# A two-block transformer on one core: scores per head on 64 rows, normalisation on VectorE, and another machine model in the scheduling pass

## The chip, the cores and the metric

The kernel runs on one core of a Trainium2 chip. The metric is the device time of the whole program in microseconds (us), measured from several runs; one further run is profiled, and the rows below come from it. The engines are TensorE (PE, with its weight loads PEld), VectorE (DVE), ScalarE (ACT), GpSimd (POOL) and SyncE (SP, which issues the DMAs). Each engine works through its own queue in order and waits on semaphores for the others.

## What is computed

256 tokens of width 1024 go through two blocks and a final norm. What matters here are the three attentions; all heads have 64 channels.

```
# block 0, NSA: 16 query heads, 4 key heads; branches: compressed, selected, window
q  = rms_norm(to_heads(q, 16), q_gain) * 64 ** -0.5
ks = rms_norm(to_heads(ks, 4), k_gain[1]); kw = rms_norm(to_heads(kw, 4), k_gain[2])
s  = einsum('bgrqd,bgqnld->bgrqnl', q, k_g) - slopes * dist     # causal, per head
p  = masked_softmax(s)
o  = gate0 * o_compressed + gate1 * o_selected + gate2 * o_window
# block 0, further: out-projection, experts (MoE), a per-layer embedding (PLE)
# block 1, moba: 16 query heads, 4 shared key heads, one softmax per head; out-projection, MoE, PLE, ffn1
# mixer: half of the width by pooling, half by 8 heads with decayed scores; ffn2; final norm
```

With 256 tokens the selected blocks and the window hold all earlier tokens, so that both branches are causal softmaxes over 256 keys with an ALiBi term.

## The kernel before

**Products.** Everything is float32. A dense layer splits each operand into a high and a low part and adds three products (`mm3`, L305 to L307: hi with hi, hi with lo, lo with hi). Weights come by DMA into tiles of the tag `raw` (9 slots), in units of at most 128x2048; `halves` splits each unit into `hi` (ScalarE, L292) and `lo` (VectorE, L293). The tag `a` names four banks of PSUM, `b` the other four; dense layers with tokens on the partitions write `a`.

**Keys.** `kb` is a tile of the tag `raw` too. In before it holds, for each of four pairs of heads, two copies of the keys of 256 tokens: one with zeros in the partitions 64 to 127 and one with zeros in 0 to 63. The zeros are written by two memsets on GpSimd (L545) when the program asks for the tile; `put_k` then writes the keys after their transposes (L348), head by head, L557 on ScalarE and L559 on VectorE.

**The way to the keys.** In NSA: the compression of keys and values (L642, then a gelu over L645 to L649, then small products L652, L666, L670 and L683), and `k_T`: squares on ScalarE (L494), sums on VectorE (L495), an inverse square root by three Newton steps on VectorE (L315 to L324), the scaling (L536), eight transposes on TensorE (L348), `put_k`. In moba the same `k_T` follows the dense layer `w_kv`. In program order `k_T` stands before the next dense layer (NSA: the window part of `w_a_in`; moba: `w_b_q`).

**One softmax** (`softmax_T`, 28 times: 16 in NSA, 8 in moba, 4 in the mixer) is two heads by 256 queries: scores for the first 128 queries against 128 keys (L566) and for the other 128 against 256 keys (L568), both heads by one product each, since the zeros of `kb` keep the heads apart; the mask and ALiBi term with the row maximum on VectorE (L575); the exponential on ScalarE (L580); the normalisation of four blocks, the first by ScalarE (L593) and three by VectorE (L595); six transposes (L599 to L601); a copy on ScalarE (L602); the products with the values (L609, L611), where the two heads write partitions 0 to 63 and 64 to 127.

**Order.** The program is written with a tile framework. A list scheduler decides the order of the instructions of every engine before the kernel runs: it plays the program on a machine model, gives tiles their slots as the program asks for them, and picks among ready instructions by priority (program order, moved forward by `ahead_by`). On the chip the queues run in that order.

**Ahead of ffn1 and ffn2** stands `modulated_T`: 16 transposes of the residual stream (L420), and two of its statistics (L421), one for each 128 tokens.

Of the kernel before, what the change touches and what calls it, by code (L numbers as in the profile page):

```python
# [8 lines left out]
F32 = mybir.dt.float32  # L9
# [3 lines left out]
AF = mybir.ActivationFunctionType  # L13
OP = mybir.AluOpType
AX = mybir.AxisListType

P = 128
T = 256
# [5 lines left out]
K = dict(  # L24
    raw=9,
    e=7,
    w4=5,
    load_at=[1, 1],
    over_at=1,
    defer=0,  # L30
    kinds='rwwrererrrrwrr',
    mid='e',
# [8 lines left out]
    fine=1,  # L41
    fmod=0,
    ada_eng='ppppvvppvvvvppvvpv',
    sw='svvv',
    hp={'rstd': 30, 'silu': 200, 'qn': 100, 'finish': 300, 'split': 60, 'gain': 200},
    keep=[0, 0],
    xlo='g',
# [150 lines left out]
class Block:  # L198
# [340 lines left out]
        for i in range(2):  # L539
            self.put_k(4 * br + 2 * i, self.transposed(kdf, i), gain)  # L540

    def keys(self):
        kb = self.raw.tile([P, 4, 2, T], F32, tag="raw", name="kb")
        for hf in range(2):
            self.nc.gpsimd.memset(kb[64 * hf:64 * hf + 64, :, 1 - hf], 0.0)  # L545
        return kb

    def put_k(self, idx, ps, gain):

        nc = self.nc  # L550
        for hf, eng in ((0, "s"), (1, "v")):
            sl = slice(64 * hf, 64 * hf + 64)
            dst = self.KB[idx // 4][sl, idx % 4:idx % 4 + 2, hf, :]
            if gain is None:
                self.copy(dst, ps[sl])
            elif eng == "s":
                nc.scalar.activation(dst, ps[sl], AF.Identity, scale=gain[sl])  # L557
            else:
                nc.vector.tensor_scalar(dst, ps[sl], gain[sl], None, op0=OP.mult)  # L559

    def softmax_T(self, j, kb, QT, slopes, dist, mult, gate):

        nc = self.nc
        with self.ahead_by("soft"):
            s0 = self.psa([P, 2, P])
            nc.tensor.matmul(s0, QT[:, j, 0:P], kb[:, :, 0:P], start=True, stop=True)  # L566
            s1 = self.psa([P, 2, T])
            nc.tensor.matmul(s1, QT[:, j, P:T], kb, start=True, stop=True)  # L568
            m = self.stat([P, 4], "m")
            p = self.pp_p.tile([P, 6 * P], F32, tag="p", name="p")  # L570
            p0, p1 = p[:, 0:2 * P].rearrange("p (h k) -> p h k", h=2), p[:, 2 * P:].rearrange("p (h k) -> p h k", h=2)
            blocks = [(p0[:, 0], s0[:, 0], P, 2 * P), (p0[:, 1], s0[:, 1], P, 2 * P),
                      (p1[:, 0], s1[:, 0], 0, 2 * P), (p1[:, 1], s1[:, 1], 0, 2 * P)]
            for i, (p, s, a, b) in enumerate(blocks):
                nc.vector.tensor_tensor_reduce(out=p, in0=s, in1=dist[:, a:b], scale=-float(slopes[2 * j + i % 2]),  # L575
                                               scalar=3e38, op0=OP.add, op1=OP.min, accum_out=m[:, i:i + 1])
            den = self.stat([P, 4], "den")
            for i, (p, s, a, b) in enumerate(blocks):
                if mult is None:
                    nc.scalar.activation(p, p, AF.Exp, bias=m[:, i:i + 1], scale=-1.0, accum_out=den[:, i:i + 1])  # L580
                else:
                    nc.scalar.activation(p, p, AF.Exp, bias=m[:, i:i + 1], scale=-1.0)
                    nc.vector.tensor_tensor_reduce(out=p, in0=p, in1=mult[:, a:b], scale=1.0, scalar=0.0,
                                                   op0=OP.mult, op1=OP.add, accum_out=den[:, i:i + 1])
            w = self.stat([P, 4], "w")
            nc.vector.tensor_scalar(den, den, 1e-30, None, op0=OP.max)
            nc.vector.reciprocal(w, den)
            if gate is not None:
                nc.vector.tensor_tensor(w.rearrange("p (t h) -> p t h", t=2), w.rearrange("p (t h) -> p t h", t=2),
                                        gate, op=OP.mult)  # L590
            for i, (p, s, a, b) in enumerate(blocks):
                if K["sw"][i] == "s":
                    nc.scalar.activation(p, p, AF.Copy, scale=w[:, i:i + 1])  # L593
                else:
                    self.engine(K["sw"][i]).tensor_scalar(p, p, w[:, i:i + 1], None, op0=OP.mult)  # L595
            pT = self.pp_p.tile([P, 2, 3 * P], F32, tag="pT", name="pT")
            for hh in range(2):
                ps = self.psb([P, 3 * P])
                nc.tensor.transpose(ps[:, 0:P], p0[:, hh], self.ident)  # L599
                nc.tensor.transpose(ps[:, P:2 * P], p1[:, hh, 0:P], self.ident)  # L600
                nc.tensor.transpose(ps[:, 2 * P:], p1[:, hh, P:T], self.ident)  # L601
                nc.scalar.activation(pT[:, hh], ps, AF.Copy)  # L602
        return pT

# [115 lines left out]
    def nsa(self):  # L720
        nc = self.nc
# [8 lines left out]
        x, = self.gained_T([self.c("first_gain")], K["head"]["nsa"])  # L730
# [30 lines left out]
        compress = self.compress(two)  # L761
        off = self.dense(x, "w_a_in", [512], put_sel, off, after=lambda: next(compress))
        next(compress)
        self.KB = [self.keys() for _ in range(2)]
        self.k_T(0, ks, self.s("a_k_norm1"))
        kw = self.w4([P, 2, 256])
        off = self.dense(x, "w_a_in", [304, 256], put_win, off)
# [2 lines left out]
        QT = self.e([P, 8, T])  # L770
# [36 lines left out]
    def moba(self):  # L807
        nc = self.nc
        xk, xq = self.gained_T([self.s("kv_norm"), self.s("ln_mix1")], K["head"]["moba"])
        r = self.rstd()  # L810
        k = self.w4([P, 2, 256])
        V = self.e([P, 2, 256])

        def put_kv(ci, t, ps):
            self.copy(k[:, t], ps[:, 0:256], r[:, t:t + 1])
            self.copy(V[:, t], ps[:, 256:512], r[:, t:t + 1])

        self.dense(xk, "w_kv", [512], put_kv, head=K["head"]["moba"])
        self.KB = [self.keys()]
        self.k_T(0, k, self.s("k_norm_shared"))  # L820
        qg = self.q_gain(self.s("b_q_norm"), self.c("qsc"))
        QT = self.e([P, 8, T])
        off = 0
        q = [self.w4([P, 2, 512]) for _ in range(2)]
        for c in range(2):
            off = self.dense(xq, "w_b_q", [512], lambda ci, t, ps: self.copy(q[c][:, t], ps, r[:, t:t + 1]), off)
            if c == 0:
                self.q_norm(q[c])
        self.q_T(QT, 0, q[0], qg)
        aT = (self.e([P, KT, T], F32R), self.e([P, KT, T], F32R))  # L830
        for j in range(8):
# [12 lines left out]
        self.moe(1, aT, "w_b_out")  # L844
# [694 lines left out]
    def mixer(self):  # L1539
        nc = self.nc  # L1540
        x = self.modulated_T(self.mods[:, 4], self.mods[:, 3], ("mixer", 0), K["head"]["mixer"])
        A = self.A["mixc"]
        o, n = self.m_at["band"]
# [9 lines left out]
        u, v = both[:, 0], both[:, 1]  # L1553
        QT = self.e([P, 4, T])
# [6 lines left out]
                nc.scalar.activation(QT[:, 2 * b + j], ps[:, j], AF.Identity, scale=self.c("qsc2", 2 * b + j, 2 * b + j + 1))  # L1561

        self.dense_T(x, "w_m_in", 4, put_q, per)
        self.KB = [self.keys()]
        self.dense_T(x, "w_m_in", 4, lambda b, ps: self.put_k(2 * b, ps, None), 2 * per)
        self.dense(x, "w_m_in", [512], lambda ci, t, ps: self.copy(v[:, t], ps), off=3 * per)
        aT = (self.e([P, KT, T], F32R), self.e([P, KT, T], F32R))
        for g in range(4):
            sl = slice(g * P, (g + 1) * P)
            ps = self.psb([P, T])  # L1570
# [4 lines left out]
            ps = self.psb([P, T])  # L1575
# [3 lines left out]
                                           op0=OP.mult, op1=OP.subtract)  # L1579
# [88 lines left out]
```

## Time and profile before

| what | value |
|---|---|
| median of 3 runs | 1143.19 us (1141.0 to 1143.75) |
| the profiled execution's own time | 1141.74 us |
| its span, first to last instruction | 1139.9 us |
| mean granted clock of TensorE | 0.973 |
| TensorE busy | 1061.5 us (93%) |
| VectorE, ScalarE, GpSimd busy | 729.1, 514.6, 74.8 us |

The stages in that execution: `w_a_in` and the compression to 84 us, NSA's attention to 157, its out-projection to 199, MoE to 320, PLE and moba's dense layers to 384, moba's attention to 414, out-projection to 450, MoE to 582, PLE to 607, ffn1 to 826, the mixer to 926, ffn2 to 1126, the final norm. Busy time of PE is modelled at the ends of products, so that a busy PE can still have room; waits are read from the time lines.

### The profile page before, as it was taken

How to read it: one execution, taken by the hardware profiler on the slowest of the kernel's cores; microseconds unless marked ns; L12 is line 12 of the kernel's file. 1: busy time of each engine (PE TensorE's matmuls, PEld its weight loads, DVE VectorE, ACT ScalarE, POOL GpSimd, SP SyncE). 2: the span in 40 equal slices, each digit the busy share in tenths (PEclk: the TensorE clock that was granted, in tenths of full speed). 3: DMA queues.
4: the chain of work that ended last, by engine and by line, in shares of the span. 5: the costliest groups of instructions: out<-in, count | busy, mean ns of one | idle time of the engine just before them, and what ended most of it. 6: DMA issues, size and time to landing. Idle time of an engine off the chain costs nothing.

```text
span 1139.9 us, 18296 instructions
## 1 busy us (share of the span) xinstructions
PE 1061.5 (93%) x7037; PEld 830.7 (73%) x7037; DVE 729.1 (64%) x1717; ACT 514.6 (45%) x992; POOL 74.8 (7%) x61
## 2 busy tenths in 40 slices
PE   7997999998899899998987999999989979999995
PEld 5884557564467667665555999999879759999994
DVE  6787866542379957343377587878674776554555
ACT  5446774221267774321253443443544634444443
POOL 3000002100010002000003000000210030000001
PEclk9998999997999999999998999999989989999998
DMA  9755464899964635898886468786674344454401
GB/s 372 287 194 223 186 231 154 300 383 371 350 245 166 245 126 187 327 372 318 333 322 265 148 239 332 302 308 252 234 300 168 129 184 145 169 189 164 141 26 38
DMA packets 46507, 268.55 MB, mean 236 GB/s; under 512 B 5328, under 2 KB 7120, under 8 KB 20432
## 3 DMA queue, kind: packets, MB, share of 16 engines
q1 hardware_dynamic: 46416, 267.34, 62.4%
q8 instruction: 57, 0.93, 0.3%
q14 instruction: 34, 0.28, 0.1%
HBM read 266.27 MB, written 1.05 MB: 235 GB/s over the span
## 4 chain that ended last, share of the span: by engine, by line
PE 47%; DVE 5%; ACT 1%; issue 0%; ACTq 0%; DVEq 0%
PE b L306 8%; PE b L305 8%; PE b L307 8%; PE a L305 5%; PE a L307 5%; PE a L306 5%; PE a L1055 1%; DVE nq L320 1%; PE b L1461 1%; DVE h L1484 1%; PE a L1095 1%; PE a L1108 1%; DVE rstd L324 1%; DVE w L1483 1%; PE b L1034 0%
## 5 line engine op out<-in xcount | busy, mean ns | idle before, releaser
L293 DVE TENSOR_TENSOR lo<-raw,hi 128x1024 fp32r<-128x1024 f32 (+2 forms) x220 | 255.9, 1167 | 166.5 <-ACT hi L292 165.7
L292 ACT ACTIVATE hi<-raw 128x1024 fp32r<-128x1024 f32 (+2 forms) x234 | 234.3, 1008 | 266.2 <-PE b L306 142.5
L305 PE MATMUL b<-e,hi 128*128 128x256 f32 x768 | 219.8, 286 | 2.9 <-ACT e L427 2.9
L306 PE MATMUL b<-e,hi 128*128 128x256 f32 x768 | 219.5, 286 | 0.1
L307 PE MATMUL b<-e,lo 128*128 128x256 f32 x768 | 219.1, 285 | 0.0
L305 PE MATMUL a<-hi,e 128*128 128x512 f32 (+2 forms) x512 | 201.5, 394 | 2.4 <-ACT e L365 1.8
L307 PE MATMUL a<-hi,e 128*128 128x512 f32 (+2 forms) x512 | 198.4, 390 | 0.5 <-DVE e L366 0.5
L306 PE MATMUL a<-lo,e 128*128 128x512 f32 (+2 forms) x512 | 198.9, 388 | 0.0
L305 PEld LDWEIGHTS b<-e,hi 128*128 128x128 f32 x768 | 149.4, 195 | 3.9 <-ACT e L427 3.6
L306 PEld LDWEIGHTS b<-e,hi 128*128 128x128 f32 x768 | 149.4, 194 | 1.0 <-DVE e L428 0.7
L307 PEld LDWEIGHTS b<-e,lo 128*128 128x128 f32 x768 | 149.3, 194 | 0.0
L305 PEld LDWEIGHTS a<-hi,e 128*128 128x128 f32 x512 | 97.4, 190 | 23.2 <-ACT e L365 2.9
L307 PEld LDWEIGHTS a<-hi,e 128*128 128x128 f32 x512 | 96.7, 190 | 21.3 <-DVE e L366 2.1
L306 PEld LDWEIGHTS a<-lo,e 128*128 128x128 f32 x512 | 97.6, 191 | 19.0 <-DVE lo L293 0.9
L1055 PE MATMUL a<-raw,e 128*32 128x256 f32 x832 | 78.6, 399 | 5.5 <-PEq L1314 5.4
L1055 PEld LDWEIGHTS a<-raw,e 128*32 128x32 f32 x832 | 32.2, 113 | 23.9 <-issue 9.0
L1439 DVE SCALAR_TENSOR_TENSOR w<-raw,c,w 128x512 f32<-128x512 f32 x63 | 45.7, 747 | 0.6
L485 DVE TENSOR_TENSOR h<-h,a 128x512 f32<-128x512 f32 x48 | 31.9, 684 | 21.0 <-PE a L1108 14.4
L580 ACT ACTIVATE p<-p,m 128x128 f32<-128x128 f32 (+1 forms) x96 | 42.6, 447 | 5.5 <-DVE m L575 4.4
L293 POOL TENSOR_TENSOR lo<-raw,hi 128x1024 fp32r<-128x1024 f32 (+1 forms) x14 | 31.4, 2263 | 206.1 <-ACT hi L292 206.0
L1098 ACT ACTIVATE w<-a,sv 128x512 fp32r<-128x512 f32 x32 | 21.6, 687 | 50.0 <-PE a L1095 49.0
L1084 ACT ACTIVATE hb<-a,rr 128x128 f32<-128x128 f32 x16 | 6.0, 373 | 83.6 <-DVE rr L1024 77.2
(321 smaller groups left out, 1455.9 us busy)
## 6 DMA issues: line engine op xcount, KB each, us to landing
raw<-in_ffn SPq DMA_DIRECT2D x62, 1024.0 KB, 4.8
raw<-in_moe_gu SPq DMA_DIRECT2D x52, 1024.0 KB, 7.3
raw<-in_w_ada SPq DMA_DIRECT2D x36, 1024.0 KB, 6.7
wd<-in_moe_dn SPq DMA_DIRECT2D x64, 512.0 KB, 6.1
raw<-in_w_gate SPq DMA_DIRECT2D x8, 1024.0 KB, 10.8
raw<-in_w_m_in SPq DMA_DIRECT2D x8, 1024.0 KB, 7.3
raw<-in_w_a_in SPq DMA_DIRECT2D x7, 1024.0 KB, 11.0
e<-in_moe_gu SPq DMA_DIRECT2D x6, 1024.0 KB, 6.7
```

The costliest lines, as they stand in the source:

```text
L292: nc.scalar.activation(hi[:, sl], raw[:, at], AF.Copy)
L293: eng.tensor_tensor(lo[:, sl], raw[:, at], hi[:, sl], op=OP.subtract)
L305: mm(out, l[0], r[0], start=start, stop=False, **kw)
L306: mm(out, l[0], r[1], start=False, stop=False, **kw)
L307: mm(out, l[1], r[0], start=False, stop=stop, **kw)
L320: nc.vector.scalar_tensor_tensor(q, y, h, y, op0=OP.mult, op1=OP.mult)
L324: nc.vector.scalar_tensor_tensor(y, q, 1.5, y, op0=OP.add, op1=OP.mult)
L485: self.nc.vector.tensor_tensor(self.h[:, t, sl], self.h[:, t, sl], ps, op=OP.add)
L580: nc.scalar.activation(p, p, AF.Exp, bias=m[:, i:i + 1], scale=-1.0, accum_out=den[:, i:i + 1])
L1055: nc.tensor.matmul(pgs[pp][32 * x:32 * x + 32], xg[:, k, o:o + 32], wg[kk][:, x], start=(k == 0), stop=(k == KT - 1))
L1098: nc.scalar.activation(yh[:, sl], py, AF.Identity, scale=cw)
L1439: eng.scalar_tensor_tensor(rows, w, by, rows, op0=OP.mult, op1=OP.add)
```

## The change

Four things change at once. (1) Scores are computed per head: a product per head and per half of the queries, on the 64 partitions of that head, heads alternating, each head into its own bank of PSUM. (2) So `kb` needs no zeros: the two memsets for each tile are gone, NSA's two tiles become one, and `put_k` is one copy of 128x512 by the engine whose turn it is. (3) All four blocks of a softmax are normalised by VectorE. (4) The scheduling pass uses its time-line machine model. Below line 545 the new file's numbers are smaller by 3 to 7.

```diff
-    sw='svvv',
+    sw='vvvv',
...
-    def keys(self):
-        kb = self.raw.tile([P, 4, 2, T], F32, tag="raw", name="kb")
-        for hf in range(2):
-            self.nc.gpsimd.memset(kb[64 * hf:64 * hf + 64, :, 1 - hf], 0.0)
-        return kb
+    def keys(self, n):
+
+        kb = self.raw.tile([P, n, 4, T], F32, tag="raw", name="kb")
+        self.KB = [kb[:, i] for i in range(n)]
 
     def put_k(self, idx, ps, gain):
 
-        nc = self.nc
-        for hf, eng in ((0, "s"), (1, "v")):
-            sl = slice(64 * hf, 64 * hf + 64)
-            dst = self.KB[idx // 4][sl, idx % 4:idx % 4 + 2, hf, :]
-            if gain is None:
-                self.copy(dst, ps[sl])
-            elif eng == "s":
-                nc.scalar.activation(dst, ps[sl], AF.Identity, scale=gain[sl])
-            else:
-                nc.vector.tensor_scalar(dst, ps[sl], gain[sl], None, op0=OP.mult)
+        dst = self.KB[idx // 4][:, idx % 4:idx % 4 + 2]
+        if gain is None:
+            self.copy(dst, ps)
+        else:
+            self.copy(dst, ps, gain)
...
-            s0 = self.psa([P, 2, P])
-            nc.tensor.matmul(s0, QT[:, j, 0:P], kb[:, :, 0:P], start=True, stop=True)
-            s1 = self.psa([P, 2, T])
-            nc.tensor.matmul(s1, QT[:, j, P:T], kb, start=True, stop=True)
+            s = [self.psa([P, 3 * P]) for _ in range(2)]
+            for t in range(2):
+                for hh in range(2):
+                    sl = slice(64 * hh, 64 * hh + 64)
+                    nc.tensor.matmul(s[hh][:, t * P:t * P + (t + 1) * P], QT[sl, j, t * P:(t + 1) * P],
+                                     kb[sl, 0:(t + 1) * P], start=True, stop=True)
...
-            for i, (p, s, a, b) in enumerate(blocks):
-                if K["sw"][i] == "s":
-                    nc.scalar.activation(p, p, AF.Copy, scale=w[:, i:i + 1])
-                else:
-                    self.engine(K["sw"][i]).tensor_scalar(p, p, w[:, i:i + 1], None, op0=OP.mult)
+            for i, (o, x, a) in enumerate(blocks):
+                self.engine(K["sw"][i]).tensor_scalar(o, o, w[:, i:i + 1], None, op0=OP.mult)
...
-        self.KB = [self.keys() for _ in range(2)]
+        self.keys(2)
         self.k_T(0, ks, self.s("a_k_norm1"))
...
-    with tile.TileContext(nc) as tc:
+    with tile.TileContext(nc, schedule_with_timeline_sim=True) as tc:
```

The order of the queues at three places. The first is the compression's end in NSA, on ScalarE's queue; `hi<-raw 128x608` and `128x512` are splits of the window part of `w_a_in`. Before:

```order
L292 ACTIVATE hi<-raw 128x608 x4
L645 ACTIVATE x_398<-b 128x256
L648 ACTIVATE x_398<-x_398 128x256
L292 ACTIVATE hi<-raw 128x512
L658 ACTIVATE w_407<-b 128x4x16
L292 ACTIVATE hi<-raw 128x512
L658 ACTIVATE w_407<-b 128x4x16
L675 ACTIVATE w_434,kcs<-b 128x64
L494 ACTIVATE w_463<-w_241 128x256
L494 ACTIVATE w_466<-w_241 128x256
L292 ACTIVATE hi<-raw 128x512
```

And now:

```order
L638 ACTIVATE x_398<-b 128x256
L641 ACTIVATE x_398<-x_398 128x256
L651 ACTIVATE w_407<-b 128x4x16 x2
L668 ACTIVATE w_434,kcs<-b 128x64
L494 ACTIVATE w_458<-w_241 128x256
L494 ACTIVATE w_461<-w_241 128x256
L665 ACTIVATE vc<-b 128x256
L262 ACTIVATE kb<-b,small 128x512
L292 ACTIVATE hi<-raw 128x608 x4
L292 ACTIVATE hi<-raw 128x512 x3
```

The first four splits stood ahead of the gelu (L645, now L638) and now stand behind the copy into kb. On TensorE's queue at the same place, where L642 (now L635) is the compression's first product, the new order is:

```order
L635 MATMUL b<-raw,e 64x256 x32
L645 MATMUL b<-consts,x_398 128x128 x2
L659 MATMUL b<-small,w_407 128x64
L663 MATMUL b<-small,w_408 128x64
L659 MATMUL b<-small,w_407 128x64
L663 MATMUL b<-small,w_408 128x64 x7
L676 MATMUL b<-consts,kd 128x128
L348 MATMUL b<-consts,w_479 128x128 x8
L305 MATMUL a<-hi,e 128x304 x2
```

In before, products `a<-hi,e` and `a<-lo,e` with 128x304 and 128x256 stood between all of these; now the first of them follows the key transposes L348.

The second place is moba, on TensorE's queue around the key transposes. Before, with products of `w_b_q` on either side:

```order
L305 MATMUL a<-hi,e 128x512
L306 MATMUL a<-lo,e 128x512
L307 MATMUL a<-hi,e 128x512
L348 MATMUL b<-consts,w_3765 128x128 x2
L305 MATMUL a<-hi,e 128x512
L306 MATMUL a<-lo,e 128x512
L348 MATMUL b<-consts,w_3765 128x128 x6
```

And now, where the three rows ahead of L348 are the last ones of `w_kv`:

```order
L305 MATMUL a<-hi,e 128x512
L306 MATMUL a<-lo,e 128x512
L307 MATMUL a<-hi,e 128x512
L348 MATMUL b<-consts,w_3786 128x128 x8
L305 MATMUL a<-hi,e 128x512 x2
```

The products of `w_b_q` that stood ahead of L348 in before (37 of them) now stand behind it.

The third place is TensorE's queue ahead of ffn1, where L1448 (now L1441) makes the modulation's vectors. Before:

```order
L1448 MATMUL b<-raw,c_701 32x512 x16
L420 MATMUL b<-consts,h 128x128 x6
L421 MATMUL a<-consts,rstd 128x128
L420 MATMUL b<-consts,h 128x128 x10
L421 MATMUL a<-consts,rstd 128x128
```

And now:

```order
L1441 MATMUL b<-raw,c_692 32x512 x11
L420 MATMUL b<-consts,h 128x128 x16
L421 MATMUL a<-consts,rstd 128x128 x2
L305 MATMUL b<-e,hi 128x256
L306 MATMUL b<-e,hi 128x256
```

The ten L420 of the second 128 tokens moved ahead of the first L421; the same happens ahead of ffn2.

## Rows read from the trace of the kernel before

**Rows 1.** The page: span and busy time of the engines.

```profile
span 1139.9 us, 18296 instructions
...
PE 1061.5 (93%) x7037; PEld 830.7 (73%) x7037; DVE 729.1 (64%) x1717; ACT 514.6 (45%) x992; POOL 74.8 (7%) x61
```

**Rows 2.** Windows: busy us of PE, PEld, DVE, ACT, POOL; clock, DMA share, GB/s.

```profile
100.00:110.00 10.00, 5.03 (x25) 3.01 (x24) 7.63 (x34) 6.60 (x19) 0.00 (x0) 0.66 0.38 129
110.00:157.00 47.00, 45.75 (x281) 25.13 (x282) 33.78 (x167) 33.69 (x116) 0.00 (x0) 1.00 0.58 220
...
385.00:415.00 30.00, 24.23 (x121) 14.87 (x123) 23.31 (x120) 23.63 (x83) 0.00 (x0) 1.00 0.68 253
884.00:908.00 24.00, 23.71 (x129) 17.21 (x128) 20.51 (x97) 16.98 (x41) 0.00 (x0) 1.00 0.27 99
```

**Rows 3.** Time line of PE, mixer scores: start us, us, line, names, count.

```profile
891.22 0.60 PE L566 MATMUL a<-kb,e 128*128 128x256 f32 x2
891.66 1.02 PE L568 MATMUL a<-kb,e 128*128 128x512 f32 x2
892.52 0.59 PE L1576 MATMUL b<-pool,w 128*128 128x256 f32 x2
```

**Rows 4.** Time line of PE: NSA's products with the values, then a wait.

```profile
98.68 0.65 PE L609 MATMUL b<-pT,e 128*64 128x256 f32 x4
99.16 0.39 PE L611 MATMUL b<-pT,e 128*64 128x128 f32 x4
...
104.75 0.48 PE L599 MATMUL b<-consts,p 128*128 128x128 f32 x1 [4.62 <-ACT p L593]
```

**Rows 5.** Time line of ACT ahead of the end of that wait.

```profile
103.36 1.04 ACT L292 ACTIVATE hi<-raw 128x1024 fp32r<-128x1024 f32 x1
104.31 0.39 ACT L593 ACTIVATE p<-p,w 128x128 f32<-128x128 f32 x1
```

**Rows 6.** Line L595: duration ns min/median/max, first and last start us, forms.

```profile
L595 DVE TENSOR_SCALAR p<-p,w x84: 257/346/350, 93.2 to 905.0; 128x256 f32<-128x256 f32 x56, 128x128 f32<-128x128 f32 x28
```

**Rows 7.** Windows, PE's products into tile a alone: busy us, count, clock.

```profile
43.30:56.90 13.60, 11.88 (x81) 1.00 1.01 420
...
361.40:369.20 7.80, 7.80 (x36) 1.00 0.71 260
```

**Rows 8.** Windows, PE's products into tile b alone: busy us, count, clock.

```profile
43.30:56.90 13.60, 3.58 (x25) 1.00 1.01 420
```

**Rows 9.** Time line at the end of the compression: start us, us.

```profile
43.40 0.38 ACT L645 ACTIVATE x<-b 128x256 f32<-128x256 f32 x1 [4.22 <-PE b L642]
...
45.12 0.42 DVE L649 SCALAR_TENSOR_TENSOR x<-x,b 128x256 f32<-128x256 f32 x1 [0.48 <-ACT x L648]
```

**Rows 10.** Groups on DVE from 43 to 58 us: busy us, mean ns.

```profile
L536 DVE TENSOR_TENSOR w<-w,knr 128x256 f32<-128x256 f32 x3 | 1.1, 419 | 0.0
L495 DVE TENSOR_REDUCE knv<-w 128x4 f32<-128x256 f32 x2 | 0.8, 414 | 0.0
...
L322 DVE TENSOR_TENSOR nq<-knr 128x8 f32<-128x8 f32 x3 | 0.5, 165 | 0.0
```

**Rows 11.** Tile kb: duration ns min/median/max, first and last start us, forms.

```profile
L557 ACT ACTIVATE kb<-b,small x6: 672/680/688, 59.1 to 371.4; 64x512 f32<-64x512 f32 x6
```

**Rows 12.** Time line at moba's keys: start us, us.

```profile
362.05 0.40 ACT L494 ACTIVATE w<-w 128x256 f32<-128x256 f32 x1
```

**Rows 13.** Windows of PE alone: busy us (count), granted clock, DMA share, GB/s.

```profile
102.00:109.00 7.00, 3.94 (x16) 0.51 0.16 26
...
931.50:942.00 10.50, 6.87 (x31) 0.51 0.56 236
```

**Rows 14.** Time line of PE ahead of ffn1.

```profile
615.08 1.21 PE L420 MATMUL b<-consts,h 128*128 128x128 f32 x9 [2.81 <-DVE w L268]
619.80 0.48 PE L421 MATMUL a<-consts,rstd 128*128 128x128 f32 x1 [3.51 <-DVE rstd L324]
```

**Rows 15.** Time line of PE ahead of ffn2.

```profile
931.07 0.32 PE L421 MATMUL a<-consts,rstd 128*128 128x128 f32 x1 [4.59 <-DVE rstd L324]
```

More of the change, by code (lines that the diff above doesn't have):

```diff
@@ L564, in softmax_T @@
         with self.ahead_by("soft"):
-            s0 = self.psa([P, 2, P])
-            nc.tensor.matmul(s0, QT[:, j, 0:P], kb[:, :, 0:P], start=True, stop=True)
-            s1 = self.psa([P, 2, T])
-            nc.tensor.matmul(s1, QT[:, j, P:T], kb, start=True, stop=True)
-            m = self.stat([P, 4], "m")
-            p = self.pp_p.tile([P, 6 * P], F32, tag="p", name="p")
-            p0, p1 = p[:, 0:2 * P].rearrange("p (h k) -> p h k", h=2), p[:, 2 * P:].rearrange("p (h k) -> p h k", h=2)
@@ L572, in softmax_T @@
-            blocks = [(p0[:, 0], s0[:, 0], P, 2 * P), (p0[:, 1], s0[:, 1], P, 2 * P),
-                      (p1[:, 0], s1[:, 0], 0, 2 * P), (p1[:, 1], s1[:, 1], 0, 2 * P)]
-            for i, (p, s, a, b) in enumerate(blocks):
-                nc.vector.tensor_tensor_reduce(out=p, in0=s, in1=dist[:, a:b], scale=-float(slopes[2 * j + i % 2]),
+            s = [self.psa([P, 3 * P]) for _ in range(2)]
[4 more added lines that the diff above has]
+                                     kb[sl, 0:(t + 1) * P], start=True, stop=True)
@@ L576, in softmax_T @@
+            m = self.stat([P, 4], "m")
+            p = self.pp_p.tile([P, 2, 3 * P], F32, tag="p", name="p")
+            blocks = [(p[:, hh, t * P:t * P + (t + 1) * P], s[hh][:, t * P:t * P + (t + 1) * P], (1 - t) * P)
+                      for t in range(2) for hh in range(2)]
+            for i, (o, x, a) in enumerate(blocks):
+                nc.vector.tensor_tensor_reduce(out=o, in0=x, in1=dist[:, a:2 * P], scale=-float(slopes[2 * j + i % 2]),
                                                scalar=3e38, op0=OP.add, op1=OP.min, accum_out=m[:, i:i + 1])
@@ L577, in softmax_T @@
             den = self.stat([P, 4], "den")
-            for i, (p, s, a, b) in enumerate(blocks):
+            for i, (o, x, a) in enumerate(blocks):
                 if mult is None:
-                    nc.scalar.activation(p, p, AF.Exp, bias=m[:, i:i + 1], scale=-1.0, accum_out=den[:, i:i + 1])
+                    nc.scalar.activation(o, o, AF.Exp, bias=m[:, i:i + 1], scale=-1.0, accum_out=den[:, i:i + 1])
                 else:
-                    nc.scalar.activation(p, p, AF.Exp, bias=m[:, i:i + 1], scale=-1.0)
-                    nc.vector.tensor_tensor_reduce(out=p, in0=p, in1=mult[:, a:b], scale=1.0, scalar=0.0,
+                    nc.scalar.activation(o, o, AF.Exp, bias=m[:, i:i + 1], scale=-1.0)
+                    nc.vector.tensor_tensor_reduce(out=o, in0=o, in1=mult[:, a:2 * P], scale=1.0, scalar=0.0,
@@ L590, in softmax_T @@
                                         gate, op=OP.mult)
-            for i, (p, s, a, b) in enumerate(blocks):
-                if K["sw"][i] == "s":
-                    nc.scalar.activation(p, p, AF.Copy, scale=w[:, i:i + 1])
-                else:
-                    self.engine(K["sw"][i]).tensor_scalar(p, p, w[:, i:i + 1], None, op0=OP.mult)
+            for i, (o, x, a) in enumerate(blocks):
+                self.engine(K["sw"][i]).tensor_scalar(o, o, w[:, i:i + 1], None, op0=OP.mult)
             pT = self.pp_p.tile([P, 2, 3 * P], F32, tag="pT", name="pT")
@@ L598, in softmax_T @@
                 ps = self.psb([P, 3 * P])
-                nc.tensor.transpose(ps[:, 0:P], p0[:, hh], self.ident)
-                nc.tensor.transpose(ps[:, P:2 * P], p1[:, hh, 0:P], self.ident)
-                nc.tensor.transpose(ps[:, 2 * P:], p1[:, hh, P:T], self.ident)
+                for k in range(3):
+                    nc.tensor.transpose(ps[:, k * P:(k + 1) * P], p[:, hh, k * P:(k + 1) * P], self.ident)
                 nc.scalar.activation(pT[:, hh], ps, AF.Copy)
@@ L818, in moba @@
         self.dense(xk, "w_kv", [512], put_kv, head=K["head"]["moba"])
-        self.KB = [self.keys()]
+        self.keys(1)
         self.k_T(0, k, self.s("k_norm_shared"))
@@ L1563, in mixer @@
         self.dense_T(x, "w_m_in", 4, put_q, per)
-        self.KB = [self.keys()]
+        self.keys(1)
         self.dense_T(x, "w_m_in", 4, lambda b, ps: self.put_k(2 * b, ps, None), 2 * per)
```

## The prediction

> **What bounds the kernel now.** I read the page first. TensorE is busy for 1061.5 of 1139.9 us, VectorE for 729.1, ScalarE for 514.6, GpSimd for 74.8 [rows 1]. So a microsecond of work taken from TensorE is worth up to a microsecond, and so is a microsecond of waiting; work added to VectorE costs only where VectorE is what TensorE waits for, and the dropped memsets on GpSimd are worth nothing by themselves. Then the windows of the three attention stages show where which of this holds [rows 2]. From 110 to 157 us (NSA) TensorE is busy for 45.75 of 47 us, from 884 to 908 us (mixer) for 23.71 of 24: it sets the pace there. From 100 to 110 us it is busy for 5.03 of 10 and its granted clock is 0.66, and from 385 to 415 us (moba) for 24.23 of 30, with VectorE at 23.31 and ScalarE at 23.63: there a chain over three engines sets the pace. Last come the time lines and the order of the queues, since the new order can open gaps where there are none.
>
> **Scores.** One softmax of before runs L566 and L568, 256 and 512 columns on 128 rows: they start at 891.22 and 891.66 us, and the next line starts at 892.52 [rows 3], so 0.44 and 0.86, together 1.30 us. The new form has 128 and 256 columns for each of two heads: again 768 columns, on half the rows. If the heads' products run one after the other, nothing is gained; the row for that is the same 1.30. No product on 64 rows of the array and 128 columns is in the trace. The nearest are L609's, on 128 rows and 64 columns, of which the two heads also alternate: four records (two products, each in two passes) start at 98.68 and the next line at 99.16 [rows 4], 0.48 us, where two serial products of 256 columns cost 2 x 0.44 = 0.88 [rows 3]. That is a ratio of 0.55, and by it the four score products take 0.71 us, a gain of 0.59. Bounds: 0 and 0.59. I take 0.55 per softmax, near the pair that I can see, less a little for 28 x 2 more weight loads.
> [...]
> NSA has 16 softmaxes: 16 x 0.55 = **-8.8**. The mixer has 4: **-2.2**. In moba, 8 softmaxes, TensorE waits for the others anyhow; I take **-1.0** of the possible 4.4.
>
> **Normalisation.** At 104.75 us the transposes L599 end a wait of 4.62 us for L593, ScalarE's normalisation [rows 4]. ScalarE was not idle: L593 started at 104.31 behind a split of weights of 1.04 us (L292) [rows 5], and other work stood ahead of that. In the new order all four blocks are normalised by VectorE, which does its blocks at 0.26 to 0.35 us each [rows 6]; that costs VectorE 28 x 0.26 = 7 us over the whole run, in NSA beside 33.78 of 47 us of its work [rows 2], so hidden there. Without this cover it would cost 4 us in NSA and 2 in moba. Of the wait at most 4.6 us come back, at least 2.4, since VectorE has 7.63 us of work in those ten [rows 2]. I take **-4.0**. The granted clock is 0.51 from 102 to 109 us [rows 13], behind that wait; half of the 3.94 us that TensorE works there, **-2.0**, comes back with it. In moba VectorE gets slower by its blocks as the ScalarE waits vanish: **-1.0**.
>
> **Keys, and what the order shows.** One copy of 128x512 takes the place of two of 64x512 (0.68 us on ScalarE, [rows 11]). The time is the same for one and VectorE loses one of two; that is hidden beside TensorE. What counts is what is no longer there: the memset was the first writer of kb, and let it have its slot of the tag raw early. Now put_k's copy is the first writer, and the order shows the splits of all later weight tiles of this tag behind that copy on ScalarE's queue. On TensorE's queue the dense products that need those splits stand behind the key transposes L348 (NSA: none is left between L642 and L348; moba: none between the dense layer w_kv and L348).
> NSA: in before, TensorE worked on dense products (tile a) for 11.88 of the 13.6 us from 43.3 to 56.9, and on the small products (tile b) for 3.58 [rows 7, 8] (their modelled ends overlap a little). After, only the latter and the transposes are left. How long is the chain to the copy? It starts at 43.40 and the gelu's last step ends at 45.12 + 0.42 = 45.54 [rows 9]. VectorE alone then has two L495 (0.8), about 12 short operations of 0.165 (2.0) and four L536 (3 in 1.1, so 1.5) [rows 10]: 49.8 with nothing in between, too short, since L652, L658, L666, L670, L494 and the transposes come between on other engines. Upper bound: before's first copy, at 59.1 us [rows 11], held up by splits on VectorE that are now behind it. I take 55.6, nearer to the top because five hand-overs lie between. The copy (0.7) and the first split (608 of 1024 columns of a 1.04 us split, [rows 5], so 0.6) bring TensorE back at 56.9. Idle: 13.6 - 3.58 - about 1.1 for eight transposes = **+8.9**; with the bounds, +3 and +12.
> The clock: behind the gaps of 4.62 and 4.59 us [rows 4, 15] the granted clock is 0.51 for 7 and 10.5 us, and half the work in them, 3.94 and 6.87 us [rows 13], is 2.0 and 3.4 us lost. A longer gap will do the same: **+2.2**.
> Moba: the last product of w_kv ends at about 361.4; the squares of the keys start at 362.05 [rows 12]. Squares 0.4, L495 0.8, short ones 2.0, L536 1.5, the transposes' tail 0.4, copy 0.7, split 1.04 [rows 5, 10, 11] bring 368.9, and the second product of each three needs the other half of the split. From 361.4 to 369.2 TensorE worked on dense products for all of 7.80 us [rows 7]; of these the eight transposes refill 1.1. I take 7.5 for the gap: **+7.5**, bounds +6 (no hand-over costs) and +10 (the splits as in before on VectorE), and **+2.2** for the clock.
> Mixer: the dense layer for v moves behind put_k too, but the pooling products cover most of it: **+1.0** (0 to 2).
>
> **The rest of the new order.** Ahead of ffn1 TensorE waits 2.81 us with L420 and 3.51 us with L421 [rows 14], and ahead of ffn2 4.59 us with L421 [rows 15]. Now all 16 L420 stand ahead of both L421 at both places. The second transpose of the statistics then waits for nothing that L420 could have covered; but the late work, the statistics on VectorE, stays. I take **-2.0**, between 0 and all of it with the clock behind it (rival C). What is moved on SP's queue in the expert layers (a few loads of down weights behind w_gate) I cost at nothing: the same tiles are asked for by the same slots.
>
> **Sum.** Gains 8.8 + 2.2 + 1.0 + 4.0 + 2.0 + 1.0 + 2.0 = 21.0; losses 8.9 + 2.2 + 7.5 + 2.2 + 1.0 = 21.8. Net +0.8 on the profiled execution's 1141.74 us, 1142.5. The median of the three runs, 1143.19, lies 1.45 above that execution, and with it the forecast would be 1144.0; I say **1143 us**, no change that can be told from none (about 0.3%, 3.4 us, is what a measurement of this kernel tells).
>
> **Rivals.**
> A, slower: the two heads' products do not run at the same time. Place: the 28 score groups; then the gain of 12.0 is lost and the time is 1155. It decides as soon as a softmax's scores take over 1.1 us instead of 0.75. For it: no 64-row product is in the trace; against it: L609's pairs.
> [...]
> B, slower: the key stops are at their upper bounds, 12 and 10 us, and the clock costs 3.4 each: 1143 + 3.1 + 2.5 + 2.4 = 1151. For it: several engines take turns there; against it: VectorE's queue holds no splits there any more.
> C, faster: the stalls ahead of ffn1 and ffn2 go (2.81 + 3.51 + 4.59 and 3.4 and 2.0 for the clock behind them are 16.3; less the 2.0 counted, 14), or half of that and key stops at their lower bounds (7 + 6 + 1.5): 1129. For it: the list of reasons is long and the order differs everywhere; against it: the statistics there hang on VectorE.
>
> **How the numbers follow.** Forecast 0.42 (own range 1137 to 1149: faster 0.09, same 0.21, slower 0.12); A 0.15 (slower 0.14, same 0.01); B 0.10 (slower 0.09, same 0.01); C 0.33 (faster 0.29, same 0.03, slower 0.01). Together faster 0.38, same 0.26, slower 0.36. The range 1126 to 1158 takes in A, B and C's point and leaves 2 in 10 outside.
>
> **What would show it.** A softmax's four products in 0.7 to 0.8 us, and no wait of L599 of over 1 us, show the gains right. Gaps on TensorE of 7 to 12 us in all around 43 to 57 us and 6 to 10 around moba's key transposes, each with a lower clock behind, show the losses right. The forecast is wrong if scores stay at 1.3 us, if dense products fill those gaps after all, or if the waits ahead of ffn1 and ffn2 go.

## The result: 1161.5 us, slower by 19

The changed kernel takes 1161.53 us (median of four runs, 1157.56 to 1163.33) against 1142.43 us for the kernel before, a ratio of 1.0163 with a 95% interval of 1.0131 to 1.0194. The forecast of 1143 us and its range, up to 1158, missed it. The profiled execution spans 1161.5 us, 21.6 more than before. Its page, for the rows that answer to [rows 1]:

```profile
span 1161.5 us, 18533 instructions
...
PE 1071.0 (92%) x7149; PEld 843.3 (73%) x7149; DVE 722.7 (62%) x1741; ACT 505.7 (44%) x960; POOL 66.3 (6%) x53
```

TensorE is busy for 9.5 us more, although the scores are cheaper: it works at the lower clock for longer. Its mean granted clock fell from 0.973 to 0.953. The clock records of both traces hold two values, 1.0 and 0.5; by that (an estimate, 2 x (1 - clock) x span) TensorE was at the lower one for 62 us before and 109 after.

Where the time goes is read by following the same work in both traces. The first product of NSA's compressed scores starts at 84.4 us before and 96.5 after (+12.1); the first expert product of the first MoE at 206.4 and 227.2 (+20.8); that MoE's last at 320.6 and 330.5 (+9.9, so the experts give 11 back); moba's first scores at 385.6 and 401.1 (+15.6); the first expert product of the second MoE at 458.6 and 486.9 (+28.3); its end at 581.7 and 606.7 (+25.0). From there to the end of the program 3.4 are won back. So there are four places: the two key stops that the order showed (NSA +12.1, moba +5.7 between the end of the experts and the scores), and the two attention stages with their out-projections (+8.7 and +12.7), for which the prediction had counted gains.

The time line of TensorE at NSA's key stop (start us, us, line, names, count, wait ahead of it and its releaser):

```profile
46.47 0.44 PE L645 MATMUL b<-consts,x 128*128 128x128 f32 x2 [2.30 <-DVE x L642]
...
48.91 3.25 PE L663 MATMUL b<-small,w 128*128 128x64 f32 x14
...
54.96 2.12 PE L348 MATMUL b<-consts,w 128*128 128x128 f32 x8 [2.29 <-DVE w L536]
57.81 0.88 PE L305 MATMUL a<-hi,e 128*128 128x304 f32 x2 [0.73 <-ACT hi L292]
```

The reader sees no dense product (`a<-hi,e`) until 57.81 us; the prediction had 56.9. The small products stretch too (L663: 14 records in 3.25 us, in before 1.67), and the granted clock is down: 0.50 from 48.4 to 61.9 us, in before 1.00 from 48.5 to 51.5, where its 14 records are. The window of that stretch (busy us of PE, PEld, DVE, ACT, POOL; clock, DMA share, GB/s):

```profile
40.00:61.00 21.00, 14.87 (x80) 11.24 (x77) 11.66 (x47) 5.64 (x14) 0.00 (x0) 0.70 0.55 207
```

In moba the same: a wait of 4.78 us ahead of the transposes, and one of 1.08 behind them for the splits.

```profile
372.92 2.12 PE L348 MATMUL b<-consts,w 128*128 128x128 f32 x8 [4.78 <-DVE w L536]
376.13 1.22 PE L305 MATMUL a<-hi,e 128*128 128x512 f32 x2 [1.08 <-ACT hi L292]
```

Now the scores of NSA. Four products of one softmax (eight records) start at 97.07 us and the next line at 97.93, and the long wait of [rows 4] is not gone but longer, on another line:

```profile
97.07 0.93 PE L565 MATMUL a<-kb,e 64*128 64x128 f32 x8
97.93 0.88 PE L691 MATMUL a<-kc,e 128*128 128x64 f32 x6
...
104.02 0.92 PE L565 MATMUL a<-kb,e 64*128 64x128 f32 x4 [0.31 <-DVE w L268]
112.90 0.69 PE L709 MATMUL b<-consts,pc 128*128 128x128 f32 x2 [7.96 <-DVE pc L707]
```

So in this softmax the heads do run at the same time: their records start 6 to 7 ns apart, and it takes 0.86 us instead of 1.30 [rows 3]. It is not so everywhere. Of the 224 records of score products in this trace 140 start within 30 ns of another one; where a head's two products stand alone, as at 162.12 us, they take 0.85 us, as long as those of both heads together. Counted from the start of the scores to the start of the next line, waits left out, they take 18.1 us in NSA (23.9 before), 10.2 in moba (10.5, but now partly at the lower clock, 0.50 from 407.0 to 423.7 us) and 4.3 in the mixer (5.2). That is about 7 us less on TensorE.

TensorE then waits 7.96 us for VectorE at the transposes of the compressed softmax. Before, the wait at the same place was 0.18 us:

```profile
91.72 0.44 PE L716 MATMUL b<-consts,pc 128*128 128x128 f32 x2 [0.18 <-DVE pc L714]
```

VectorE is not idle in that time. In the changed kernel three splits of weights (L293) stand on its queue ahead of the compressed softmax's last step (L707); in before there is none between the first compressed score and that step (L714).

```profile
107.36 1.23 DVE L293 TENSOR_TENSOR lo<-raw,hi 128x1024 fp32r<-128x1024 f32 x1 [0.28 <-ACT hi L292]
...
111.28 1.22 DVE L293 TENSOR_TENSOR lo<-raw,hi 128x1024 fp32r<-128x1024 f32 x1
112.42 0.42 DVE L707 TENSOR_TENSOR pc<-pc,wc 128x256 f32<-128x256 f32 x1
```

So from the first compressed score to these transposes it takes 16.4 us instead of 7.3, and the order on VectorE's queue has its part in that. The windows of the attention stages, to be set beside [rows 2], show a lower clock in each:

```profile
100.00:150.00 50.00, 38.54 (x257) 23.57 (x255) 39.77 (x178) 28.97 (x90) 0.00 (x0) 0.83 0.57 218
380.00:430.00 50.00, 45.83 (x224) 32.45 (x222) 35.76 (x129) 28.82 (x76) 0.00 (x0) 0.83 0.63 234
```

### The profile page after: what moved, and what is told of

It reads as the page before. It is cut to its first block, busy times and chain, and to the rows that moved or that the text cites. A ratio compares the mean times of both kernels' runs of the same rounds, so it can differ in the third digit from the quotient of the medians.

```text
span 1161.5 us, 18533 instructions
## 1 busy us (share of the span) xinstructions
PE 1071.0 (92%) x7149; PEld 843.3 (73%) x7149; DVE 722.7 (62%) x1741; ACT 505.7 (44%) x960; POOL 66.3 (6%) x53
## 4 chain that ended last, share of the span: by engine, by line
PE 46%; DVE 5%; ACT 1%; issue 1%; DVEq 0%; ACTq 0%
PE b L306 8%; PE b L305 8%; PE b L307 8%; PE a L305 5%; PE a L307 5%; PE a L306 5%; PE a L1048 1%; DVE h L1477 1%; PE b L1454 1%; PE a L1088 1%; DVE w L1476 1%; PE a L1101 1%; DVE nq L320 1%; DVE w L1402 0%; PE a L565 0%
## 5 line engine op out<-in xcount | busy, mean ns | idle before, releaser
L293 DVE TENSOR_TENSOR lo<-raw,hi 128x1024 fp32r<-128x1024 f32 (+2 forms) x220 | 255.2, 1163 | 193.7 <-ACT hi L292 185.0
L305 PE MATMUL a<-hi,e 128*128 128x512 f32 (+2 forms) x512 | 194.8, 394 | 2.8 <-ACT hi L292 1.8
L307 PE MATMUL a<-hi,e 128*128 128x512 f32 (+2 forms) x512 | 195.8, 390 | 0.0
L1048 PE MATMUL a<-raw,e 128*32 128x256 f32 x832 | 68.3, 383 | 1.1 <-DVEq L1285 0.8
L293 POOL TENSOR_TENSOR lo<-raw,hi 128x1024 fp32r<-128x1024 f32 (+1 forms) x14 | 32.6, 2342 | 385.7 <-ACT hi L292 356.0
L1092 DVE SCALAR_TENSOR_TENSOR w<-a,sv,w 128x512 fp32r<-128x512 f32 x32 | 24.0, 750 | 34.5 <-ACT w L1091 33.5
L1101 PE MATMUL a<-w,GT 128*128 128x512 f32 x128 | 38.9, 420 | 7.1 <-ACT w L1091 3.8
L1048 PEld LDWEIGHTS a<-raw,e 128*32 128x32 f32 x832 | 28.4, 109 | 23.1 <-issue 5.1
L1088 PE MATMUL a<-wd,hT 128*32 128x512 f32 x256 | 40.3, 613 | 2.1 <-ACT hT L1083 2.1
```

What stands on the lines that cost most here:

```text
L293: eng.tensor_tensor(lo[:, sl], raw[:, at], hi[:, sl], op=OP.subtract)
L305: mm(out, l[0], r[0], start=start, stop=False, **kw)
L307: mm(out, l[1], r[0], start=False, stop=stop, **kw)
L1048: nc.tensor.matmul(pgs[pp][32 * x:32 * x + 32], xg[:, k, o:o + 32], wg[kk][:, x], start=(k == 0), stop=(k == KT - 1))
L1088: nc.tensor.matmul(py[32 * x:32 * x + 32], hT[:, 32 * x:32 * x + 32], wd[2 * n + x // 2][:, x % 2], start=True, stop=True)
L1092: nc.vector.scalar_tensor_tensor(yl[:, sl], py, cw, yh[:, sl], op0=OP.mult, op1=OP.subtract)
```

## The experiments

Three theories went in. Theory 1: the key stops carry the loss. Theory 2: the order that the time-line machine makes of the attention stages carries it. Theory 3: the 64-row products themselves lower the granted clock in attention. Every edit changes the scheduler's order elsewhere too, so a few us can come from there. All results, with the mean granted clock of the profiled run:

| run | edit against | median us | ratio to before [95%] | clock |
|---|---|---|---|---|
| before | | 1142.4 | 1 | 0.973 |
| changed kernel | before | 1161.5 | 1.0163 [1.0131, 1.0194] | 0.953 |
| e1 time-line machine alone | before | 1154.3 | 1.0101 [1.0075, 1.0127] | 0.963 |
| e2 default machine | changed | 1170.5 | 1.0243 [1.0226, 1.0260] | 0.960 |
| e3 kb early | changed | 1141.8 | 0.9992 [0.9973, 1.0011] | 0.962 |
| e4 kb early, default machine | changed | 1145.8 | 1.0028 [1.0018, 1.0038] | 0.970 |
| e5 normalisation alone | before | 1144.0 | 1.0021 [1.0010, 1.0031] | 0.970 |
| e6 e4, first block on ScalarE | e4 | 1148.1 | 1.0055 [1.0038, 1.0072] | 0.966 |
| e7 e3, first block on ScalarE | e3 | 1132.6 | 0.9910 [0.9893, 0.9926] | 0.970 |
| e8 kb early in NSA alone | changed | 1149.3 | 1.0063 [1.0039, 1.0088] | 0.963 |
| e9 two key tiles in NSA | e7 | 1137.4 | 0.9960 [0.9948, 0.9972] | 0.975 |
| e10 two blocks on ScalarE | e7 | 1134.4 | 0.9920 [0.9900, 0.9940] | 0.968 |
| e11 scores head by head | e7 | 1132.0 | 0.9911 [0.9895, 0.9928] | 0.976 |
| e12 scores twice | e7 | 1136.4 | 0.9958 [0.9944, 0.9972] | 0.983 |
| e13 scores twice | changed | 1158.5 | 1.0151 [1.0125, 1.0178] | 0.974 |
| e14 scores twice | e3 | 1136.9 | 0.9949 [0.9932, 0.9966] | 0.985 |
| e15 first block on ScalarE | changed | 1157.5 | 1.0119 [1.0101, 1.0137] | 0.959 |

**e1 and e2: the machine model alone, and everything but it.** The edit is the last one of the change, made or undone by itself.

```diff
-    with tile.TileContext(nc) as tc:
+    with tile.TileContext(nc, schedule_with_timeline_sim=True) as tc:
```

> The kernel before with the time-line machine alone; kb, scores and normalisation as before. Theory 1 (the key stops carry the loss): the memset is there, so no key stop, 1143 +- 4. Theory 2 (the time-line order of the attention stages carries the loss: NSA's attention ended 8.7 us later than its start explains, moba's 12.8): 1150 to 1160, with waits of over 2 us on the compressed transposes and a half clock in moba's attention. Theory 3 (products on 64 rows lower the granted clock in attention): no such products here, 1143 +- 4 and the clock of before.

> The changed kernel with the default machine. Theory 1: the key stops stay, about 12 us in NSA and 8 in moba, less what the expert layers give back and the gains of scores and normalisation: 1143 to 1155. Theory 2: NSA's and moba's attention are no longer late, so 1138 to 1150, at least 8 us under the changed kernel. Theory 3: about 1160, the clock in attention low as in the changed kernel.

Measured: 1154.3 and 1170.5. By itself the time-line order costs 11.9 us, as theory 2 has it; but taken from the changed kernel it costs 9 more, which no theory had. The model's worth depends on the program that it orders.

**e3 and e4: kb early.** One column of kb is set on GpSimd at the place of the old memsets; that is all that is brought back of them.

```diff
         kb = self.raw.tile([P, n, 4, T], F32, tag="raw", name="kb")
+        self.nc.gpsimd.memset(kb[:, 0, 0, 0:1], 0.0)
         self.KB = [kb[:, i] for i in range(n)]
```

> The changed kernel, but one column of kb is set on GpSimd when the program asks for the tile, so that kb has its slot early and the splits behind it are not held back. Theory 1: both key stops go, 1140 to 1147. Theory 2: they go, but the attention stages are late by the time-line order as before, 1148 to 1156. Theory 3: as theory 2.

> As the run before, on the default machine. Theories 1 and 2 together: no key stops and the old order's attention, with scores and normalisation gained: 1125 to 1135, faster than both kernels. Theory 3: the attention keeps its low clock, 1140 or more.

Measured: 1141.8, 19.7 us under the changed kernel, and 1145.8, 24.7 us under e2. The time line of TensorE in e3 at the place where the changed kernel stood still has dense products behind the compression at once:

```profile
44.45 0.41 PE L305 MATMUL a<-hi,e 128*128 128x304 f32 x1
44.70 0.30 PE L306 MATMUL a<-lo,e 128*128 128x304 f32 x1
```

The first compressed scores start at 85.1 us (before 84.4, changed 96.5). This shows the key stops and their cause, the late slot. It also shows that all the rest of the change is worth nothing: 1141.8 against 1142.4, and on the default machine even 3.4 us lost. The stages show where the gains went. From the first compressed score to the first expert product e3 takes 129.8 us, before 122.0; from moba's first scores to the second MoE's first expert product 84.8, before 73.0. So both attention stages are late without the key stops too, and on the default machine as well (e4: 131.3 and 77.0). In NSA's, TensorE idles for 14.8 us in e3 (before 8.8) and is at the lower clock for 13.7 (6.8); in moba's it idles for 9.3 (7.3) and is at the lower clock for 23.9, before not at all. It is won back elsewhere: 11.9 us in the first MoE (102.3 against 114.2), where a wait of 5.13 us in before and the lower clock behind it (0.50 from 266.0 to 279.4 us) are missing. Theory 1 is right on the loss, and the gains are missing.

**e8: which stop.** As e3, but only where two branches share the tile (`if n == 2`), so in NSA alone.

> The changed kernel with kb set early in NSA alone; moba and the mixer keep their key stops. If the stops add up (12 us in NSA and 8 in moba of the 19.7 that both gave back): about 1150. If the expert layers behind NSA take up what comes early there: 1155 to 1160, and the moba stop is worth most of the 19.7.

Measured: 1149.3. NSA's stop was worth 12.2 us of the 19.7, moba's and the mixer's together 7.5.

**e5, e6, e7 and e15: normalisation and scores apart.** In e5 `sw` alone becomes 'vvvv' on the kernel before; in e6, e7 and e15 it goes back.

```diff
-    sw='vvvv',
+    sw='svvv',
...
+                if K["sw"][i] == "s":
+                    nc.scalar.activation(o, o, AF.Copy, scale=w[:, i:i + 1])
+                else:
+                    self.engine(K["sw"][i]).tensor_scalar(o, o, w[:, i:i + 1], None, op0=OP.mult)
```

> The kernel before with all four blocks normalised by VectorE, nothing else. If the wait of 4.62 us for ScalarE and the half clock behind it come back as forecast: 1133 to 1138. If VectorE then ends the same wait a little earlier (the chain over three engines is the bound), or the expert layers take the gain up: 1140 to 1143.

> Default machine, scores per head, one column of kb set early, the first block still normalised by ScalarE. If the gain of 0.55 us per softmax is there: about 1131. If it is eaten by what the run with the default machine showed (products of the two heads apart from each other, and about 0.1 us more at each change between 64 and 128 rows): 1140 to 1147, with the scores' slots on TensorE near 1.2 us per softmax.

> As the run with kb early on the time-line machine (1141.8), but the first block normalised by ScalarE. If the normalisation on VectorE helps under this order too: 1145 to 1150. If it does not matter there: 1142 +- 3.

> The changed kernel with the first block normalised by ScalarE as in before. If the normalisation's 9 us add to the key stops: 1150 to 1155. If the key stops leave VectorE free enough: 1161 +- 4.

Measured: 1144.0, 1148.1, 1132.6, 1157.5. The normalisation on VectorE costs 1.6 us alone, 9.2 with kb early (e7 to e3) and 4.1 in the changed kernel (e15 to it, at the edge of the intervals); on the default machine with kb early it gains 2.3 (e6 to e4, at the edge as well). In e5 the wait of [rows 4] is there still, shorter and with another releaser; the waits of TensorE from 84 to 215 us (us, times, longest):

```profile
PE b L599 <- DVE p L595: 3.8, 2, 2.8
PE b L609 <- ACT pT L602: 1.5, 4, 0.6
```

In e6 the scores take 1.25 us per softmax on TensorE in NSA (before 1.49) and 1.15 in the mixer (1.29), since many heads' products stand apart; so over the program only about 3 us were taken off TensorE there. And e7 is faster than both kernels, by 9.8 us than before: scores per head, kb early, time-line machine, first block on ScalarE. It was the best found, with e11.

**e9: a slot more or less.** Two tiles for NSA's keys, as before, each half as long, in e7.

```diff
-        kb = self.raw.tile([P, n, 4, T], F32, tag="raw", name="kb")
-        self.nc.gpsimd.memset(kb[:, 0, 0, 0:1], 0.0)
-        self.KB = [kb[:, i] for i in range(n)]
+        self.KB = []
+        for i in range(n):
+            kb = self.raw.tile([P, 4, T], F32, tag="raw", name="kb")
+            self.nc.gpsimd.memset(kb[:, 0, 0:1], 0.0)
+            self.KB.append(kb)
```

> The best kernel so far (scores per head, kb early, time-line machine, first block on ScalarE; 1132.6), but NSA's keys in two tiles of the tag raw instead of one, each half empty. The first expert stage of before, and of the runs with the time-line machine alone and with the normalisation alone, has a half clock of 13.7 to 17.1 us near 266 to 276 us, behind a wait of about 5 us for weights; the kernels with one tile have none. If the slot that one tile frees carries this: the stretch returns and the time is 1137 to 1143. If not: 1133 +- 3.

Measured: 1137.4, in the range of the first case, but not for its reason: the stretch of low clock in the first MoE does not return (clock 1.00 there, wait 0.84 us), and that stage takes as long as in e7. The loss comes in NSA's attention, whose first expert product starts 6.2 us later. The theory of the freed slot, as a cure of that wait, fell.

**e10 and e11.** `sw='ssvv'`, and the two loops of the score products exchanged (heads outside), both in e7.

> The best kernel so far with two of four blocks normalised by ScalarE instead of one. If VectorE is what the chain of the attention stages waits for: 1124 to 1131. If ScalarE's queue (its splits of weights) then makes the transposes wait as in the kernel before: 1133 to 1140.

> The best kernel so far, but the four score products in the order head 0, head 0, head 1, head 1, so that fewer of them run beside one of the other head. If the gain of the scores on the path is their running at the same time: 0.2 to 0.3 us per softmax less of it, 1135 to 1141. If the score products are hidden behind the chain on VectorE anyhow: 1133 +- 3.

Measured: 1134.4 (unchanged within the intervals: no gain from a second block on ScalarE) and 1132.0. E11 tells nothing: in its trace the products of the two heads still start 13 to 14 ns apart in the first softmaxes, since the scheduler put them side by side again.

**e12, e13 and e14: every score product twice.** The second writes the same values again. This adds work to TensorE alone, but the scheduler orders the program anew.

```diff
-            for t in range(2):
+            for t in (0, 1, 0, 1):
                 for hh in range(2):
```

> The best kernel so far (1132.6) with every score product issued twice, with nothing else changed; the second writes the same values again. It prices score work under this order. If scores are on the path in all 28 softmaxes: 28 x 0.76 us more, 1154. If they lie beside the chain on VectorE and ScalarE in part of them: 1138 to 1148, that is 0.2 to 0.55 us per softmax. If hidden: 1133 +- 3, and then the time that the 64-row form saves cannot be the reason for the gain over the kernel with the time-line machine alone.

> The changed kernel with every score product issued twice. If lost clock in the attention stages is what eats the scores' gain: 1158 to 1166, no more than 5 us over the changed kernel's 1161.5, with less time at half clock than its 111.7 us. If score work is on the path in this kernel: 1172 to 1182 and the half clock as before.

> The changed kernel with kb early (1141.8), every score product issued twice. If the normalisation on VectorE costs 9 us there through the clock (89.8 us at half clock against 70.0 without it): the doubled scores hold the clock up and the time stays at 1142 +- 4, the half clock falls to under 75. If VectorE's work itself is the cost: 1146 to 1155.

Measured: 1136.4, 1158.5 and 1136.9. Some 21 us of added work (28 x 0.76; in the traces the scores take 20 to 22 us more) cost 3.7 us in e7, cost nothing in the changed kernel (3.1 us less, inside the intervals) and made e3 *faster*, by 4.9 us. The windows of e3 and then of e14, from 96 to 108 us in NSA and from 376 to 460 around moba's attention, show the clock:

```profile
96.00:108.00 12.00, 6.65 (x31) 4.57 (x31) 10.91 (x42) 6.78 (x17) 0.00 (x0) 0.57 0.66 244
...
376.00:460.00 84.00, 74.27 (x382) 54.46 (x381) 53.39 (x225) 43.69 (x125) 6.16 (x5) 0.87 0.48 180
```

```profile
96.00:108.00 12.00, 8.36 (x55) 5.26 (x56) 12.00 (x51) 10.64 (x28) 0.00 (x0) 1.00 0.68 252
...
376.00:460.00 84.00, 76.78 (x490) 60.15 (x492) 57.43 (x240) 46.14 (x130) 6.63 (x6) 0.98 0.54 198
```

In NSA with the scores once, TensorE waits 7.85 us ahead of the compressed transposes, at 93.5 to 101.4 us, and is granted 0.57 in this window; with the scores twice that wait is 0.99 us and the clock 1.00. In the changed kernel the doubled scores do the same to the two windows shown with the result, 0.83 and 0.83:

```profile
100.00:150.00 50.00, 45.31 (x335) 29.89 (x336) 39.40 (x182) 29.44 (x94) 0.00 (x0) 1.00 0.62 233
380.00:430.00 50.00, 46.65 (x284) 35.78 (x283) 37.96 (x130) 28.84 (x75) 0.00 (x0) 0.99 0.64 237
```

The wait of 7.96 us at the compressed transposes is nearly gone in e13 (us, times, longest):

```profile
PE b L709 <- DVE pc L707: 1.5, 2, 1.0
```

But the added work did not do this alone. In the changed kernel and in e3 three splits of weights stand on VectorE's queue ahead of the compressed softmax's last step, in e7 two; in e12, e13 and e14 none does, they follow it. So in NSA the wait went with a new order on VectorE as well. Nor was time won there: from the first compressed score to the first expert product e14 takes 133.0 us and e3 129.8, e13 133.0 and the changed kernel 130.7. The gain lies in moba: from its first scores to the second MoE's first expert product e14 takes 78.4 us and e3 84.8, e13 78.5 and the changed kernel 85.8. There TensorE idles for 7.2 us in e14 and 9.3 in e3, which is not enough for the 6.4 us, but it is at the lower clock for 3.4 us instead of 23.9. One order by itself goes the same way: in the ten executions of e3 the time goes with the mean granted clock, from 1137.4 and 1137.5 us at 0.970 to 1146.8 at 0.957.

With the scores twice, the normalisation on VectorE costs 0.5 us (e12 to e14) instead of 9.2. Whether its price came with the clock or with the order (two splits ahead and a wait of 6.14 us in e7, three and 7.85 in e3) these runs do not part.

## Why the prediction was wrong

The forecast was 18.5 us too low. The losses came, 19.7 of the 21.8; of the 21.0 us of gains nothing is left (e3 stands 0.6 us under before).

**The key stops: right.** Forecast 8.9 and 2.2 for NSA, 7.5 and 2.2 for moba, 1.0 for the mixer, 21.8 in all; measured 19.7 (e3), of which 12.2 in NSA and 7.5 behind it (e8). The chain, the resume at 56.9 us (57.81) and the lower clock (0.50 from 48.4 to 61.9 us) came as read from the order and the rows.

**The scores' gain of 12.0: the step that failed.** Its first half, that the heads run at the same time, held in part. Where a softmax's four products stand together they take 0.86 us against 1.30, which is 0.44 saved, not 0.55; but only 140 of 224 records run beside another, and TensorE was saved about 7 us in all. Its second half, that TensorE sets the pace in NSA and the mixer, so that a microsecond saved there is one gained, was read from a busy share of 45.75 in 47 us [rows 2]. Against it stand e12, where doubled scores cost 3.7 us in place of 21, and e13 and e14, where they cost nothing. What the runs showed in its place: the stages got longer. NSA's, from the first compressed score to the first expert product, takes 130.7 us (e3: 129.8) instead of 122.0, moba's 85.8 (e3: 84.8) instead of 73.0. TensorE, done sooner, waits for VectorE: 7.96 us where the new order has splits of weights ahead of the compressed softmax's last step, and on the default machine, where none stands there, 5.1 us in all for the row maximum and 4.2 for the normalisation (e4). Around the wait of 7.96 us its clock was 0.50, from 106.4 to 116.5 us. E6 (5.7 us over before) says less, since the scores saved only some 3 us of TensorE's time there. That the busy share was high in before because the slow scores filled the time in which the chain ran is a reading that no run here shows.

**The normalisation's gain of 7.0: failed too.** The wait of 4.62 us did end with L593 on ScalarE, but VectorE ended it 1.8 us sooner, not 4 (e5); the mean granted clock did not rise with it (0.970, before 0.973). The cost on VectorE, taken as hidden in NSA and outweighed by 1.0 in moba, was 4.1 us in the changed kernel (e15 to it) and 9.2 with kb early (e7 to e3).

**The rest of the new order, -2.0.** At the two places the size was right: from the first L420 to the last L421 it takes 1.0 us less ahead of ffn1 and 1.4 less ahead of ffn2. But the prediction took these for all that the time-line machine does, beside the key stops; by itself it costs 11.9 us (e1), and it saves 15.5 with scores per head, kb early and the first block on ScalarE (e6 to e7). In e1 5.7 of the 17 us that part it from e9 lie in NSA's attention, and 7.4 in the first MoE, where a wait for weights of 2.85 us and a half clock behind it (13.7 to 17.1 us in before, e1 and e5) stand, as in before (5.13 us), and not in e9 (0.84 us, clock 1.00). Why the weights come later there was not settled. E1 and e9 differ by the form of the scores and keys alone: under the time-line machine that form, with the order that it brings, is worth 16.9 us; on the default machine, with one key tile, it costs 5.7 (before to e6). Its worth hangs on the order, and the prediction priced it without one.

Of the rivals, A named the right term: the heads overlap in part only, and the gain is lost beyond that. B's longer key stops and C's cured waits did not come. Theory 3 fell: with more 64-row products the clock was higher (0.974 in e13 against 0.953, 0.985 in e14 against 0.962). Theory 2 fell as stated: the attention stages are late on the default machine too (e4), and the time-line order is bad for one program and good for the other. What is shown: the late slot costs 19.7 us, score work taken from TensorE or added to it does not come out in the time one for one, and the attention stages are late and at a lower clock. Not shown is how the missing gains divide between VectorE's order, the clock behind TensorE's waits and the scheduler's order elsewhere, because every edit, the doubled scores too, changed the order with it.

## What to carry to other kernels

A store that looks useless may be what places a tile: before a memset is dropped, look in the new order at what is queued behind the tile's next first writer. A busy share near 1 does not show that an engine sets the pace when the work fills waits of a chain; issue that work twice, and see what it costs, before taking time out of it; and look in the traces at what the scheduler moved for it on the other engines, or an effect of the order passes for one of the work. And when TensorE waits, read the queue of the engine that it waits for: here splits of weights stood ahead of the step that would have ended the wait.

## What the runs showed of the hardware

TensorE was granted less clock where it had waited longer: in e3, with a wait of 7.85 us, 0.57 from 96 to 108 us; in e14, with a wait of 0.99 us there, 1.00. Issuing 21 us of score products twice took 4.9 us off a kernel (e3 to e14, 1141.8 to 1136.9 us), with the mean granted clock of the profiled execution up from 0.962 to 0.985; the order changed too, so that the clock's share of the 4.9 is open.

The changes between products on 64 and on 128 rows took time in the changed kernel's trace. The first score pair of a softmax, of 128 columns, starts at 97.07 us and its second pass at 97.29, 0.21 us, where that second pass is followed after 0.11. The last one starts at 97.62, and L691, on 128 rows, at 97.93, 0.31 us, where products of 256 columns on 64 rows otherwise follow each other in 0.22 (97.40 to 97.62). By these starts about 0.1 us (an estimate) went to each of the two changes, in and out, 0.2 of the 0.86.
